# A decoder layer step on one core: the decay's columns loaded once, sums by one product, and the past rows of the FFN in small loads

## The chip, the cores and the metric

The kernel runs on one core of a Trainium2 chip. A core has a matrix engine (TensorE, PE in the profile, with its weight loads shown apart as PEld), a vector engine (VectorE, DVE), a scalar engine (ScalarE, ACT), a general engine (GpSimd, POOL) and a sync engine (SP) that here only issues transfers. Each engine runs its instructions in the order in which they stand in its queue, and waits on semaphores where it needs another engine's result or a transfer. Transfers run on 16 DMA engines and are issued from the queues of SP, POOL and ACT. The metric is the time of one execution on the device in microseconds; the kernel before has a median of 2003.5 us over three runs.

## What is computed

One layer of a hybrid decoder for two request groups that share the weights: a prompt of 256 tokens and 8 samples of one token each, 264 columns together, with a model width of 2048. The reference, cut to what matters here:

```python
proj = jnp.einsum('bld,de->ble', x, w_in)
q, k, v, g, a_lr, cb, cc, ch, mq, z_a, z_b, z_m = jnp.split(proj, SPLIT_POINTS, axis=-1)
log_a = jax.nn.log_sigmoid((a_lr @ w_gla_a2 + b_gla_a2).astype(f32)) / GLA_GATE_NORM   # decay, rank 16
o, s_gla_new = _gla_recurrence(qh, kh, vh, log_a..., s_gla)          # 4 heads, state 256 x 512 each
...
u, s_conv_new = _causal_dwconv(cc * ch, s_conv, w_conv)
...
logits = jnp.einsum('blhd,bmhd->bhlm', qm, mem_k) * (MEM_HD ** -0.5) # 256 memory tokens, 4 heads
p = jax.nn.softmax(logits, axis=-1)
om = jnp.einsum('bhlm,bmhd->blhd', p, mem_v)
...
x = _layer_norm(DN_ALPHA * x + merged @ w_o, ln1_g, ln1_b)
hg = x @ w_ffn_gate; hu = x @ w_ffn_up
hc, s_new = _causal_dwconv(hg, s_ffn, w_ffn_conv, b_ffn_conv)        # s_ffn: 2 past rows of 5504 per sample
x = _layer_norm(DN_ALPHA * x + (jax.nn.silu(hc) * hu) @ w_ffn_down, ln2_g, ln2_b)
```

For the prompt the memory's keys and values are computed from `mem_prompt` and are outputs as well; for the samples they come from a cache, and so do the state of the linear attention and the past rows of the convolutions.

## The kernel before

The activations stand transposed: 128 features on the partitions, 264 tokens along the free dimension. Every float32 operand is split in a high and a low part of a shorter format (fp32r), and a product is made as three: high by high, high by low, low by high (L302, L303, L304). `group` (L280) computes 512 output columns from 16 tiles of 128 input features. Its weights come in tiles of 128 x 1024 values (512 KB): `granule` (L260) loads one on SP's queue into one of four buffers `ws`, ScalarE rounds it to `wh` and VectorE subtracts to `wl` (L277), three buffers each. A `ws` buffer is free for the next load when VectorE has made `wl`; a `wh` buffer when TensorE is through with it. A granule of `group` holds 24 products.

Beside this stream other work is threaded in. `put` queues a unit with its load (one sample's cache or state) and its work; `tick` runs at the end of each granule, counts a clock, runs what `later(n, f)` put off by n ticks, and takes units from the queue. A scheduler then orders each engine's instructions by priorities. `issue_after` orders two instructions on one engine without making one wait for the other.

In order of time, the stages that the change and the prediction speak of:

- **Start.** `constants` (L123) builds on POOL, among other things, `strip`, a table of 32 x 32 identities from which `quads(c)` takes 128 columns.
- **Memory keys and values** (L510 to L542). Two products of the prompt's memory, 512 columns at a time (L520 to L522). Beside them run the samples' key units (`key_unit`, L425): each loads a cache tile of 512 KB and a query row that is spread over 128 partitions from `dq` in DRAM (256 KB), and VectorE multiplies and sums them in four instructions (L439). The results go out on POOL (L529).
- **Attention of the prompt over the memory** (L547 to L578), in two halves of two heads (`c`), each in two tiles of tokens (`lt`): logits on TensorE (L554), maximum and its scaling on VectorE (L557, L558), exponentials on ScalarE (L561), reciprocal and division on VectorE (L563, L564), four transposes on TensorE (L568), then the products with the values (L575).
- **The decay's columns.** `w_in` has 16 columns for the decay (`A0`, with the 16 next to them loaded too). The group at L591 takes them three times, so that the three parts of the second product stand on partitions 0 to 31, 32 to 63 and 64 to 95: three loads of 128 KB for each half of the 2048 features, 48 products of 96 columns. `aT` and `wa2` hold the operands of the second product (L620), 96 partitions each.
- **Samples' sums** (`sum_rows`, L459). For values and for each head's state, VectorE transposes and reduces blocks of 32 x 32 for each of 8 samples into `R`, then `product` adds over the partitions: four products of 32 columns with `quads` (L473) and one copy (L474). This happens six times. `own_key` (L635) sums over 256 channels in two products (L638), once for each head.
- **The FFN's past rows** (L1055 to L1068). `fr`, 86 partitions of 8 x 128, is loaded by POOL in two loads of 172 KB each (L1059): for each of the two past rows, 43 partitions of 8 samples by 128 values. POOL issues them ahead of its next work, in the stage with the `w_conv_out` products (about 850 us). `turn_fpast` turns them on TensorE (L1064) during the products with `w_o`, 20 and 24 ticks after these start.

The order around the change is set by SP's queue (all weight tiles, units and query rows in one line), by VectorE's queue (splits of weights, key units and the softmax in one line), and by which buffers are free.

Of the kernel before, what the change touches and what calls it, by code (L numbers as in the profile page):

```python
# [17 lines left out]
P = 128  # L18
# [16 lines left out]
def layer_kernel(ctx, tc, x_prompt, x_sample, mem_prompt, cache_mem_k, cache_mem_v, state_gla, state_conv,  # L35
# [81 lines left out]
    strip = sb.tile([P, 7 * 32], F32, name="strip")  # L117
    vcol = sb.tile([P, NV], F32, name="vcol")
    fcol = sb.tile([P, 172], F32, name="fcol")

    quads = lambda c: strip[:, 96 - 32 * c:224 - 32 * c]

    def constants():  # L123
        G.memset(strip, 0.0)
        for a in range(4):
            G.tensor_tensor(strip[:, 96:128], strip[:, 96:128], ident[:, 32 * a:32 * a + 32], ALU.add)
# [332 lines left out]
    def sum_rows(sums, b, z, dst, after=None):  # L459
# [9 lines left out]
        def product():  # L469
            pt = small()  # L470
            o = pt[:, 0:4 * NS].rearrange("p (b j) -> p b j", b=NS)
            for c in range(4):
                T.matmul(o, quads(c), R.rearrange("p b (j c) -> p b j c", c=4)[:, :, :, c], start=(c == 0), stop=(c == 3))  # L473
            V.tensor_copy(dst() if callable(dst) else dst, pt[:, 0:4 * NS].rearrange("p (b j) -> p j b", b=NS))  # L474
            if after:
                after()
# [32 lines left out]
    for name, w, dst in (("k", w_mem_k[0], o_mk), ("v", w_mem_v[0], o_mv)):  # L509
# [18 lines left out]
        for m in range(2):  # L528
            G.dma_start(dst[0, 0, m * P:(m + 1) * P].rearrange("m h d -> m (h d)"), mt_[m])  # L529
# [48 lines left out]
    flush()  # L578
# [7 lines left out]
    wr = big(F32, (96, 1024))  # L586
    wa2 = big(F32R, (96, 1024))
    G.memset(wr, 0.0)
    for i in range(3):
        G.dma_start(wr[32 * i:32 * i + 16], w_gla_a2[0])  # L590
    pa, = group([(win, A0, 32)] * 3, 16, xh, xl, gk=8)  # L591
    aT = sb.tile([96, NT], F32R, name="aT")
    S.copy(aT, pa[0:96])
# [17 lines left out]
    def head(h, q, k, vf):  # L611
# [16 lines left out]
        def decays_of_samples():  # L628

            S.activation(eas[:, h], la[:, :, NP:NT], AF.Exp, scale=1.0 / 16.0)  # L630
            dot = tiny((P, 2, NS))
            V.tensor_mul(dot, qks[:, 0, h], qks[:, 1, h])
            later(1, lambda: (V.tensor_mul(qas[:, h], qks[:, 0, h], eas[:, h]), own_key(dot)))

        def own_key(dot):  # L635
            pz = small()
            for kt in range(2):
                T.matmul(pz[:, 0:NS], onesm, dot[:, kt], start=(kt == 0), stop=(kt == 1))  # L638
# [419 lines left out]
    for u in range(2):  # L1058
        G.dma_start(fr[u * NF:(u + 1) * NF], state_ffn_conv[0, :, u].rearrange("b (k f) -> k b f", f=P))  # L1059
# [7 lines left out]
    later(20, lambda: turn_fpast(0))  # L1067
    later(24, lambda: turn_fpast(4))  # L1068
# [333 lines left out]
```

## Time and profile before

| | |
|---|---|
| runs of before | 2004.73, 2000.65, 2003.50 us; median 2003.5 |
| the profiled execution | 2005.06 us, of which the profile's span is 2003.3 us |
| mean granted clock of TensorE | 0.996 |
| DMA | 439 MB in 235199 packets, mean 219 GB/s |
| SP's queue | 426.86 MB, 68.9% of 16 engines |
| POOL's queue | 8.79 MB, 1.3% of 16 engines |
| products of `group`, all three kinds | 14688, of 284 to 287 ns each, which overlap |
| splits of weights (L277) | 651 on ACT, 1039 ns each; 651 on DVE, 1234 ns each |

The profile is of one execution. A row of a timeline gives the start and the length of an instruction in us, its engine, line, operation and operands, and in brackets how long its engine stood idle before it and what ended that. A row of the table of waits reads: engine, operand and line, then what it waited for, the total in us, how often, and the longest. "Granted clock" is the share of full speed that TensorE was given in a stretch. The mean lengths of products overlap, so the time that one costs is read from how many start in a stretch.

### The profile page before, as it was taken

What the parts mean: (1) busy time and instruction counts of PE and PEld (TensorE: products, weight loads), DVE (VectorE), ACT (ScalarE), POOL (GpSimd) and SP (SyncE); (2) the same over time, 40 slices, a digit from 0 to 9 for tenths busy, and PEclk for the clock granted to TensorE, in tenths of its full rate; (3) what the DMA queues carried; (4) which work ended last, traced back from release to release, by engine and by line L of the source; (5) the groups of instructions that cost most, each with busy time, mean ns of one, the idle gap of its engine ahead of it and who ended that gap; (6) DMA issues with size and microseconds to landing.
All of it is one profiled execution on the core that took longest, in us unless ns stands there. A gap on an engine that the chain in (4) does not pass through costs nothing.

```text
span 2003.3 us, 38161 instructions
## 1 busy us (share of the span) xinstructions
PE 1984.9 (99%) x15721; PEld 1950.6 (97%) x15721; DVE 1296.7 (65%) x1947; ACT 986.3 (49%) x1348; POOL 164.1 (8%) x240
## 2 busy tenths in 40 slices
PE   9998999999999999999999999999999999999998
PEld 9887999999999999999999998999999999999997
DVE  5675866566676867865444787666665556666655
ACT  4433654454554555554444346555554445555533
POOL 4000030021310211100000201000000000000100
PEclk9999999999999999999999999999999999999999
DMA  8895866566666667866555567877777787777753
GB/s 282 272 316 189 274 201 198 176 211 197 189 190 195 201 190 241 259 173 183 179 179 181 178 213 252 256 236 231 233 246 249 259 254 238 232 233 247 237 177 119
DMA packets 235199, 439.00 MB, mean 219 GB/s; under 512 B 22862, under 2 KB 29571, under 8 KB 234889
## 3 DMA queue, kind: packets, MB, share of 16 engines
q1 hardware_dynamic: 229120, 426.86, 68.9%
q0 software_dynamic: 5040, 8.79, 1.3%
q8 instruction: 123, 2.02, 0.4%
q10 hardware_dynamic: 864, 0.92, 0.1%
q14 instruction: 52, 0.42, 0.1%
HBM read 409.76 MB, written 26.90 MB: 218 GB/s over the span
## 4 chain that ended last, share of the span: by engine, by line
PE 72%; DVE 1%; ACT 0%; issue 0%; DVEq 0%; ACTq 0%
PE mm L303 23%; PE mm L302 23%; PE mm L304 23%; PE sm L803 1%; PE sm L679 0%; PE sm L781 0%; DVE G L935 0%; PE sm L473 0%; PE sm L1276 0%; DVE wl L277 0%; PE sm L849 0%; PE sm L783 0%; PE bank L1331 0%; PE mm L1139 0%; ACT wh L277 0%
## 5 line engine op out<-in xcount | busy, mean ns | idle before, releaser
L277 DVE TENSOR_TENSOR wl<-ws,wh 128x1024 fp32r<-128x1024 f32 (+2 forms) x651 | 802.6, 1234 | 582.0 <-ACT wh L277 580.2
L277 ACT CAST wh<-ws 128x1024 fp32r<-128x1024 f32 (+2 forms) x651 | 676.1, 1039 | 878.0 <-PE mm L303 770.0
L302 PE MATMUL mm<-XH,wh 128*128 128x264 f32 (+1 forms) x2064 | 592.8, 287 | 1.8 <-ACT wh L277 1.0
L303 PE MATMUL mm<-XL,wh 128*128 128x264 f32 (+1 forms) x2064 | 588.8, 286 | 0.0
L304 PE MATMUL mm<-XH,wl 128*128 128x264 f32 (+1 forms) x2064 | 586.2, 285 | 0.7 <-DVE wl L277 0.7
L302 PE MATMUL mm<-T,wh 128*128 128x264 f32 x1456 | 415.1, 285 | 0.0
L303 PE MATMUL mm<-T,wh 128*128 128x264 f32 x1456 | 414.2, 284 | 0.0
L304 PE MATMUL mm<-T,wl 128*128 128x264 f32 x1456 | 413.8, 284 | 0.0
L302 PEld LDWEIGHTS mm<-XH,wh 128*128 128x128 f32 (+1 forms) x2064 | 390.0, 189 | 2.7 <-ACT wh L277 1.2
L302 PE MATMUL mm<-X1H,wh 128*128 128x264 f32 x1376 | 391.5, 284 | 0.0
L303 PE MATMUL mm<-X1L,wh 128*128 128x264 f32 x1376 | 391.1, 284 | 0.0
L304 PE MATMUL mm<-X1H,wl 128*128 128x264 f32 x1376 | 391.0, 284 | 0.0
L303 PEld LDWEIGHTS mm<-XL,wh 128*128 128x128 f32 (+1 forms) x2064 | 389.4, 189 | 0.5 <-DVE XL L317 0.2
L304 PEld LDWEIGHTS mm<-XH,wl 128*128 128x128 f32 (+1 forms) x2064 | 387.8, 188 | 1.2 <-DVE wl L277 1.0
L302 PEld LDWEIGHTS mm<-T,wh 128*128 128x128 f32 x1456 | 274.1, 188 | 0.1
L303 PEld LDWEIGHTS mm<-T,wh 128*128 128x128 f32 x1456 | 274.0, 188 | 0.1
L304 PEld LDWEIGHTS mm<-T,wl 128*128 128x128 f32 x1456 | 273.8, 188 | 0.0
L302 PEld LDWEIGHTS mm<-X1H,wh 128*128 128x128 f32 x1376 | 259.4, 189 | 0.2 <-issue 0.2
L303 PEld LDWEIGHTS mm<-X1L,wh 128*128 128x128 f32 x1376 | 259.0, 188 | 0.2 <-DVE T L1160 0.2
L304 PEld LDWEIGHTS mm<-X1H,wl 128*128 128x128 f32 x1376 | 258.4, 188 | 0.0
L1080 POOL DMA_DIRECT2D out_dram<-S x2 | 1.1, 551 | 637.2 <-DVE S L1077 637.2
L521 PE MATMUL mm<-wl,T 128*128 128x512 f32 x128 | 50.6, 395 | 0.0
(363 smaller groups left out, 1485.7 us busy)
## 6 DMA issues: line engine op xcount, KB each, us to landing
ws<-in_w_in_dram SPq DMA_DIRECT2D x255, 512.0 KB, 4.0
ws<-in_w_ffn_down_dram SPq DMA_DIRECT2D x84, 512.0 KB, 4.8
ws<-in_w_ffn_gate_dram SPq DMA_DIRECT2D x80, 512.0 KB, 4.4
ws<-in_w_ffn_up_dram SPq DMA_DIRECT2D x80, 512.0 KB, 4.7
S<-in_state_gla_dram SPq DMA_DIRECT2D x64, 512.0 KB, 5.3
ws<-in_w_gla_out_dram SPq DMA_DIRECT2D x32, 512.0 KB, 3.7
ws<-in_w_o_dram SPq DMA_DIRECT2D x32, 512.0 KB, 4.2
out_dram<-S SPq DMA_DIRECT2D x32, 512.0 KB, 4.2
```

Of the source, the lines that this page charges most:

```text
L277: split_at[:] = [S.copy(wh, st).ins, V.tensor_sub(wl, st, wh.bitcast(F32)).ins]
L302: T.matmul(p, wh[:, t, cs], xh(kt), start=(kt == 0), stop=False)
L303: T.matmul(p, wh[:, t, cs], xl(kt), start=False, stop=False)
L304: i = T.matmul(p, wl[:, t, cs], xh(kt), start=False, stop=(kt == nk - 1))
L521: T.matmul(pts[m], a, wl[:, t], start=False, stop=False)
L803: T.matmul(pt, kd[:, st, kt * P:(kt + 1) * P], vt[:, st], start=(st == 0), stop=(st == 1))
L1080: G.dma_start(o_pffn[0, 0, u].rearrange("(k f) -> k f", f=P), rows[:, 0])
```

## The change

The decay's columns are loaded once for each half of the features (two loads of 128 KB in place of six). ScalarE writes the high part three times side by side, VectorE the low part as a fourth block of 32 columns. A tile of features then takes two products: the 128 columns by the high part of x, and the first 96 by its low part. `aT` and `wa2` have 128 partitions, and `wr` is loaded a fourth time.

In `sum_rows` one product of 128 columns, with a table `modulo` of four identities side by side, replaces the four; four copies, on DVE and ACT in turn, pick each group of 32 partitions out of its result. `modulo` is built by VectorE from `ident`, and `strip` with its work on POOL goes. `own_key` adds its two halves on VectorE and makes one product.

The past rows are loaded on SP: sixteen loads of 43 rows of 512 B, for one sample and one past row each, two of them behind each of eight weight tiles from the first `w_o` group on, and they are turned 14 and 18 ticks after its start. The memory's keys and values are written 2 and 8 ticks later (`later`), and the loop after the attention empties the queue of units alone.

```diff
-    strip = sb.tile([P, 7 * 32], F32, name="strip")
+    modulo = sb.tile([P, 4, 32], F32, name="modulo")
-    quads = lambda c: strip[:, 96 - 32 * c:224 - 32 * c]
     def constants():
-        G.memset(strip, 0.0)
-        for a in range(4):
-            G.tensor_tensor(strip[:, 96:128], strip[:, 96:128], ident[:, 32 * a:32 * a + 32], ALU.add)
+        i4 = ident.rearrange("p (a i) -> p a i", a=4)
+        V.tensor_add(modulo[:, 0:2], i4[:, 0:2], i4[:, 2:4])
+        V.tensor_add(modulo[:, 3], modulo[:, 0], modulo[:, 1])
+        V.tensor_copy(modulo[:, 0:3], modulo[:, 3:4].to_broadcast([P, 3, 32]))
...
         def product():
             pt = small()
-            o = pt[:, 0:4 * NS].rearrange("p (b j) -> p b j", b=NS)
+            T.matmul(pt[:, 0:P], modulo.rearrange("p a i -> p (a i)"), R.rearrange("p b c -> p (b c)"),
+                     start=True, stop=True)
+            d = dst() if callable(dst) else dst
             for c in range(4):
-                T.matmul(o, quads(c), R.rearrange("p b (j c) -> p b j c", c=4)[:, :, :, c], start=(c == 0), stop=(c == 3))
-            V.tensor_copy(dst() if callable(dst) else dst, pt[:, 0:4 * NS].rearrange("p (b j) -> p j b", b=NS))
+                own = pt[32 * c:32 * c + 32, 0:P].rearrange("p (b j c) -> p j b c", b=NS, c=4)[:, :, :, c]
+                (S.copy if c % 2 else V.tensor_copy)(d[32 * c:32 * c + 32], own)
...
         for m in range(2):
-            G.dma_start(dst[0, 0, m * P:(m + 1) * P].rearrange("m h d -> m (h d)"), mt_[m])
+            later(2 + 6 * m, lambda dst=dst, mt_=mt_, m=m: G.dma_start(
+                dst[0, 0, m * P:(m + 1) * P].rearrange("m h d -> m (h d)"), mt_[m]))
...
-    flush()
+    while queue:
+        pop()
...
-    wr = big(F32, (96, 1024))
-    wa2 = big(F32R, (96, 1024))
+    wr = big(F32, (P, 1024))
+    wa2 = big(F32R, (P, 1024))
     G.memset(wr, 0.0)
-    for i in range(3):
+    for i in range(4):
         G.dma_start(wr[32 * i:32 * i + 16], w_gla_a2[0])
-    pa, = group([(win, A0, 32)] * 3, 16, xh, xl, gk=8)
-    aT = sb.tile([96, NT], F32R, name="aT")
-    S.copy(aT, pa[0:96])
+    pa = ps.tile([P, 512], F32, tag="mm", bufs=5, name=nm("mm"))[:, :NT]
+    for g in (0, 8):
+        lead[0] += 1
+        with tc.high_priority(offset=700):
+            st = sb.tile([P, 8, 32], F32, tag="ws", bufs=4, name=nm("ws"))
+            staged[:] = [nc.sync.dma_start(
+                st, win[g * P:(g + 8) * P, A0:A0 + 32].rearrange("(k p) c -> p k c", p=P)).ins]
+        with tc.high_priority(offset=450):
+            wa = sb.tile([P, 8, P], F32R, tag="wh", bufs=3, name=nm("wh"))
+            split_at[:] = [S.copy(wa[:, :, 0:96].rearrange("p k (a c) -> p k a c", a=3),
+                                  st.unsqueeze(2).to_broadcast([P, 8, 3, 32])).ins,
+                           V.tensor_sub(wa[:, :, 96:P], st, wa[:, :, 0:32].bitcast(F32)).ins]
+        for t in range(8):
+            kt = g + t
+            if kt:
+                T.matmul(pa[0:96], wa[:, t, 0:96], xl(kt), start=False, stop=False)
+            i = T.matmul(pa, wa[:, t], xh(kt), start=(kt == 0), stop=(kt == 15))
+            if kt == 0:
+                T.matmul(pa[0:96], wa[:, t, 0:96], xl(kt), start=False, stop=False)
+        last_mm[:] = [i.ins]
+        tick(1 - g // 8, 2)
+    aT = sb.tile([P, NT], F32R, name="aT")
+    S.copy(aT, pa)
...
+            V.tensor_add(dot[:, 0], dot[:, 0], dot[:, 1])
...
-            for kt in range(2):
-                T.matmul(pz[:, 0:NS], onesm, dot[:, kt], start=(kt == 0), stop=(kt == 1))
+            T.matmul(pz[:, 0:NS], onesm, dot[:, 0], start=True, stop=True)
...
-    for u in range(2):
-        G.dma_start(fr[u * NF:(u + 1) * NF], state_ffn_conv[0, :, u].rearrange("b (k f) -> k b f", f=P))
+    def load_fpast(b):
+        with tc.issue_after(staged[0]):
+            for u in range(2):
+                nc.sync.dma_start(fr[u * NF:(u + 1) * NF, b], state_ffn_conv[0, b, u].rearrange("(k f) -> k f", f=P))
+    for b in range(NS):
+        later(1 + b, lambda b=b: load_fpast(b))
...
-    later(20, lambda: turn_fpast(0))
-    later(24, lambda: turn_fpast(4))
+    later(14, lambda: turn_fpast(0))
+    later(18, lambda: turn_fpast(4))
```

Three queues at the end of the memory's values, as the built programs have them. First SP, from the last weight tile of the memory's values (`ws_1635`, after the change `ws_1633`) to the query row of the last key unit (`T_292`); tiles of 128x8x32 are the decay's columns, `S` is a key unit's cache tile. Before:

```order
L270 DMA ws_1635<-in_w_mem_v_dram 128x2x512
L430 DMA T_263_1445<-dq 128x512
L270 DMA ws_1786<-in_w_in_dram 128x8x32 x3
L428 DMA S_282_1531<-in_cache_mem_k_dram 128x2x512
L270 DMA ws_1818<-in_w_in_dram 128x8x32 x3
L270 DMA ws_1866<-in_w_in_dram 128x2x512
L430 DMA T_283_1533<-dq 128x512
L270 DMA ws_1896<-in_w_in_dram 128x2x512
L428 DMA S_291_1561<-in_cache_mem_k_dram 128x2x512
L270 DMA ws_1926<-in_w_in_dram 128x2x512
L270 DMA ws_1974<-in_w_in_dram 128x2x512
L430 DMA T_292_1563<-dq 128x512
```

After:

```order
L269 DMA ws_1633<-in_w_mem_v_dram 128x2x512
L429 DMA T_263_1442<-dq 128x512
L601 DMA ws_1783<-in_w_in_dram 128x8x32
L427 DMA S_282_1529<-in_cache_mem_k_dram 128x2x512
L429 DMA T_283_1531<-dq 128x512
L601 DMA ws_1804<-in_w_in_dram 128x8x32
L427 DMA S_291_1559<-in_cache_mem_k_dram 128x2x512
L269 DMA ws_1842<-in_w_in_dram 128x2x512
L429 DMA T_292_1561<-dq 128x512
```

The last query row stands behind one large weight tile where it stood behind four, and behind two of the narrow loads where there were six.

Second VectorE, from the key unit with `T_283` to the reciprocal of the first softmax tile or as far as twelve rows go; `ls` takes a key unit's sums, `wl` is the low part of a weight tile, `ty` the softmax's maximum, `sm_1662` and `sm_1658` its logits. Before:

```order
L439 SCALAR_TENSOR_TENSOR T_302_1607,ls<-S_282_1531,T_283_1533 128x256
L557 TENSOR_REDUCE ty_1667<-sm_1662 128x2
L439 SCALAR_TENSOR_TENSOR T_306_1627,ls<-S_291_1561,T_292_1563 128x256
L439 SCALAR_TENSOR_TENSOR T_307_1629,ls<-S_291_1561,T_292_1563 128x256
L439 SCALAR_TENSOR_TENSOR T_308_1631,ls<-S_291_1561,T_292_1563 128x256
L439 SCALAR_TENSOR_TENSOR T_309_1633,ls<-S_291_1561,T_292_1563 128x256
L558 TENSOR_SCALAR ty_1667<-ty_1667 128x2
L277 TENSOR_TENSOR wl_1899<-ws_1896,wh_1898 128x1024
L563 RECIPROCAL ty_1667<-ty_1667 128x2
```

After:

```order
L607 TENSOR_TENSOR wh_1785<-ws_1783,wh_1785 128x8x32
L438 SCALAR_TENSOR_TENSOR T_306_1625,ls<-S_291_1559,T_292_1561 128x256
L438 SCALAR_TENSOR_TENSOR T_307_1627,ls<-S_291_1559,T_292_1561 128x256
L438 SCALAR_TENSOR_TENSOR T_308_1629,ls<-S_291_1559,T_292_1561 128x256
L438 SCALAR_TENSOR_TENSOR T_309_1631,ls<-S_291_1559,T_292_1561 128x256
L607 TENSOR_TENSOR wh_1806<-ws_1804,wh_1806 128x8x32
L529 COPY T_215_1265<-mm_1465 128x512
L276 TENSOR_TENSOR wl_1845<-ws_1842,wh_1844 128x1024
L560 TENSOR_REDUCE ty_1663<-sm_1658 128x2
L561 TENSOR_SCALAR ty_1663<-ty_1663 128x2
L276 TENSOR_TENSOR wl_1875<-ws_1872,wh_1874 128x1024
L566 RECIPROCAL ty_1663<-ty_1663 128x2
```

The last key unit stood between the softmax's maximum and its scaling; it now stands ahead of the second split of the decay's columns (`wh_1806`), of the copy of the memory's values and of the whole softmax.

Third TensorE, from the last decay products (`mm_1785`, after the change `mm_1782`) to the logits of the second softmax tile; `mm_1862` and `mm_1838` to `mm_1840` belong to the first group of q. Before:

```order
L304 MATMUL mm_1785<-XH,wl_1823 96x264
L302 MATMUL mm_1862<-XH,wh_1868 128x264
L568 MATMUL sm_1675<-ident,T_320_1670 128x128 x4
L554 MATMUL sm_1681<-T_209_1243,T_46_428 128x256 x4
L303 MATMUL mm_1862<-XL,wh_1868 128x264
```

After, from the last three of the thirteen products that now stand there:

```order
L302 MATMUL mm_1839<-XL,wh_1844 128x264
L303 MATMUL mm_1839<-XH,wl_1845 128x264
L301 MATMUL mm_1840<-XH,wh_1844 128x264
L571 MATMUL sm_1671<-ident,T_320_1666 128x128 x4
L557 MATMUL sm_1677<-T_209_1239,T_46_428 128x256 x4
```

Between the decay's products and the softmax's transposes stood one product of the group of q; now there are thirteen.

## The prediction

> **What bounds the kernel now.** I read the page's busy times and its chain first, to see which engine sets the end.
>
> ```profile
> span 2003.3 us, 38161 instructions
> PE 1984.9 (99%) x15721; PEld 1950.6 (97%) x15721; DVE 1296.7 (65%) x1947; ACT 986.3 (49%) x1348; POOL 164.1 (8%) x240
> PE 72%; DVE 1%; ACT 0%; issue 0%; DVEq 0%; ACTq 0%
> ```
>
> TensorE is busy for 1984.9 of 2003.3 us, and the chain that ended last is nearly all TensorE. So an edit can pay in two ways only: fewer TensorE instructions, or a shorter stall out of the 18.4 us in which PE is idle. The table of windows says where those are.
>
> ```profile
> 120.00:200.00 80.00, 73.19 (x397) 64.15 (x396) 47.23 (x111) 28.25 (x49) 3.48 (x6) 0.96 0.73 233
> 1240.00:1900.00 660.00, 660.00 (x5426) 660.00 (x5425) 402.99 (x593) 344.82 (x486) 7.28 (x8) 1.00 0.78 243
> 1980.00:2004.00 24.00, 15.89 (x111) 13.22 (x109) 11.48 (x32) 6.00 (x15) 0.00 (x0) 0.83 0.27 91
> ```
>
> The columns are the stretch, its length, busy time (count) of PE, weight loads, DVE, ACT and POOL, then granted clock, DMA share, GB/s. From 1240 to 1900 nothing is idle: 660 us / 5426 = 0.1216 us for one product of 264 columns, the price of a TensorE instruction below. 8.1 us are idle in the tail, which the change does not touch, 6.8 between 120 and 200. The waits of PE name the causes.
>
> ```profile
> PE sm L568 <- ACT wh L277: 6.3, 1, 6.3
> PE mm L302 <- ACT wh L277: 1.0, 1, 1.0
> PE mm L304 <- DVE wl L277: 0.7, 1, 0.7
> ```
>
> One wait of 6.3 us stands at the softmax of the memory attention (about 161 to 167). The other two are one stall of 1.7 us at 873.5 to 876. The change works at both.
>
> **The decay's columns: products.** The group of L591 ran 48 products.
>
> ```profile
> 154.65 0.47 PE L302 MATMUL mm<-XH,wh 128*96 128x264 f32 x1
> 160.57 0.28 PE L304 MATMUL mm<-XH,wl 128*96 128x264 f32 x1
> ```
>
> 47 steps in 5.92 us are 0.126 us each, so 96 columns cost about what 128 do. 32 products remain: 16 x 0.1216 = **-1.95 us**. The wider aT, wa2 and the fourth POOL load lie on engines that are idle there.
>
> **The decay's columns: the 6.3 us stall.** Releasers are inferred, so I looked for what was late.
>
> ```profile
> 139.10 2.77 SPq L270 DMA_DIRECT2D ws<-in_w_in_dram  x3
> 142.59 5.72 SPq L270 DMA_DIRECT2D ws<-in_w_in_dram  x4
> 152.81 0.46 SPq L430 DMA_DIRECT2D T<-dq  x1
> 143.41 1.22 DVE L277 TENSOR_TENSOR wl<-ws,wh 128x1024 fp32r<-128x1024 f32 x1 [1.54 <-ACT wh L277]
> 153.22 0.42 DVE L439 SCALAR_TENSOR_TENSOR T<-S,T 128x256 f32<-128x256 f32 x1 [0.26 <-DMA T<-dq]
> 154.88 1.23 DVE L277 TENSOR_TENSOR wl<-ws,wh 128x1024 fp32r<-128x1024 f32 x1 [0.88 <-ACT wh L277]
> 163.57 0.42 DVE L439 SCALAR_TENSOR_TENSOR T<-S,T 128x256 f32<-128x256 f32 x1 [6.18 <-DMA T<-dq]
> 164.96 0.16 DVE L558 TENSOR_SCALAR ty<-ty 128x2 f32<-128x2 f32 x1
> 165.16 0.47 ACT L561 ACTIVATE T<-sm,ty 128x256 f32<-128x256 f32 x1 [6.24 <-DVE ty L558]
> 167.25 1.09 PE L568 MATMUL sm<-ident,T 128*128 128x128 f32 x4 [6.28 <-ACT wh L277]
> ```
>
> The last key unit's query row (dq) was issued at 152.81 and landed at 163.5, 10.7 us later. VectorE waited 6.18 us for it with the softmax (L558) queued behind; then ScalarE, then TensorE. On SP that load stood behind several large weight tiles, and the last two of these had to wait for buffers. The order now puts it behind one, ws_1842, whose buffer is freed by the split of ws_1607, the row at 143.41, which ends at 144.6. So it is issued at about 145.1, 7.7 us sooner. Its landing takes between 4.9 us (issued at the end of the x4 row, 148.3; waited for until 153.2) and 10.7 us: at 150.0 or 155.8. I take 150, as four of the six narrow loads ahead are gone. The last key unit's 1.5 us and both small splits (L607) are then done by about 152, before TensorE needs the second one (154.65 + 16 x 0.12 = 156.6).
>
> What is late next: the softmax itself. The split at 154.88 ends at 156.1. Reduction 0.7, then 2.3 (from the scale at 164.96 to the transposes at 167.25), then 1.6 more, since an exponential and a weight cast of 1.05 now stand between the two halves: transposes at 160.7. TensorE arrives there at 154.65 + 45 x 0.1216 = 160.1 (32 decay and 13 further products). 0.6 us are left, and by the same count 0.5 at the second tile. Stall: -6.3 + 1.1 = **-5.2 us**. The stall also halved the clock:
>
> ```profile
> 166.00:168.00 2.00, 0.76 (x4) 0.79 (x5) 1.06 (x3) 1.38 (x4) 0.00 (x0) 0.52 1.02 343
> 168.00:170.00 2.00, 2.00 (x7) 1.64 (x6) 1.63 (x2) 0.00 (x0) 0.00 (x0) 0.50 0.86 294
> 170.00:172.00 2.00, 2.00 (x8) 1.64 (x7) 0.41 (x2) 0.00 (x0) 0.00 (x0) 0.50 0.39 67
> 172.00:174.00 2.00, 2.00 (x15) 2.00 (x15) 1.07 (x3) 0.78 (x3) 0.00 (x0) 0.77 0.60 214
> ```
>
> 2 x (0.48 + 0.50 + 0.50 + 0.23) = 3.4 us, less 0.6 for the idle part of the first row: **-2.8 us**.
>
> **Samples' sums and own keys.**
>
> ```profile
> 579.70 0.82 PE sm L473 x8
> 576.32 0.44 PE sm L679 x4
> 657.21 0.34 PE sm L638 x4
> ```
>
> Each of six sums drops from four products (0.82) to one of 128 x 128, half of the second row: 0.22. 6 x 0.60 = **-3.6 us**. The four own keys halve the third row: 4 x 0.17 = **-0.7 us**. DVE pays four small adds and 12 copies, ACT 12 copies. Each costs about 0.2 us (a copy below); DVE is 65% and ACT 49% busy, so at nothing, until a copy holds up a weight cast.
>
> ```profile
> 881.35 0.19 DVE L474 COPY T<-sm 128x32 f32<-128x32 f32 x1 [2.61 <-PE sm L473]
> 1129.90 1.05 ACT L277 CAST wh<-ws 128x1024 fp32r<-128x1024 f32 x1 [1.90 <-PE mm L303]
> ```
>
> In the worst case a copy waits 2.6 us on ACT as here; a cast is made two tiles (5.8 us) before TensorE needs it and with its split takes 2.3, so 3.5 us are spare.
>
> **The FFN's past rows.** Their two POOL loads explain the stall at 873. First row: the two loads. Second: weight loads issued from 849 to 873. Third: weight loads of w_o, 1110 to 1160, undisturbed.
>
> ```profile
> S<-in_state_ffn_conv_dram POOLq DMA_DIRECT2D x2, 172.0 KB, 19.5
> ws<-in_w_in_dram SPq DMA_DIRECT2D x7, 512.0 KB, 11.8
> ws<-in_w_o_dram SPq DMA_DIRECT2D x16, 512.0 KB, 4.2
> 873.90:877.00 3.10, 1.50 (x6) 1.29 (x7) 2.11 (x3) 2.42 (x3) 0.00 (x0) 0.85 0.08 29
> 877.00:880.00 3.00, 3.00 (x18) 3.00 (x17) 1.67 (x2) 0.48 (x1) 0.00 (x0) 0.59 0.89 224
> ```
>
> While they run, weights take 11.8 us instead of 4.2. From 873.9 to 877 the DMA share is 0.08, about one engine of 16, at 29 GB/s (26 in a steady slice): one engine still owes its part of a weight tile, and TensorE waits. The loads leave this place, so **-1.7 us** stall and, from the clocks 0.85 and 0.59, 3.1 x 0.15 + 3.0 x 0.41 = **-1.7 us**.
>
> They come back as 16 loads of 43 rows of 512 B on SP, two behind each of eight w_o tiles from about 1126. What one costs no row shows. Two rows bound it: POOL's loads alone (853.75 to 856.5), and 128-byte pieces on SP's queue (146.5 to 149); packets, MB, share of 16 engines.
>
> ```profile
> q0 software_dynamic: 391, 0.06, 17.7%
> q1 hardware_dynamic: 1544, 0.20, 55.6%
> ```
>
> POOL's two loads kept 0.177 x 16 = 2.8 engines busy, 20 ns a packet, of which the two loads need 1376 (two to a row): 40 ns x 43 = 1.7 us a load if it runs on one engine. From below, 22 KB at 26 GB/s is 0.85. Between: 14.4 ns for 128 B (second row) and 79 ns for 2 KB at 26 GB/s give 27 ns for 512 B, 1.2 us a load. I take 1.2, since that row is of the same queue. Per w_o tile (24 x 0.1216 = 2.92 us) one engine would then carry 2.4 us of past rows and 1.26 of weights (32.8 KB at 26 GB/s), 0.7 too much, 5.9 us over eight tiles. Cover: a buffer comes free 9.4 us before its next cast (four tiles less 2.3) and the load takes 4.2, so 5.2, plus the 3.5 above: 8.7. So nothing; at 1.7 us a load it is 14 - 8.7 = 5 us of stall. A rule of the Trainium skill speaks against the change here: "DMA: Bandwidth & Descriptors", section "Why a DMA increments its semaphore by 16 and not by 1", says that a load is split over as many engines, up to 16, as divide its slowest dimension on both sides, and that on SP's queue these are the lowest-numbered ones; 43 gives one, the same for all sixteen loads. The share of 2.8 engines for two loads is nearer to that than to 16 each, and no run here shows which engine SP takes; by the rule rival 1 is what threatens, and without it (loads on several engines) there is no lag at all. The sum is the same by both.
>
> **At nothing.** The shorter turn (14, 18 ticks), the output loads put off by `later` (POOL's order is the same as before, and its waits too), and the table built on DVE, which waits there anyway:
>
> ```profile
> 6.00 0.89 DVE L317 TENSOR_TENSOR XL<-sm,XH 128x512 fp32r<-128x512 f32 x2 [4.37 <-ACT XH L317]
> ```
>
> **Sum.** 1.95 + 5.2 + 2.8 + 3.6 + 0.7 + 3.4 = 17.65 us. The profiled execution took 2005.06 us, 1.56 above the median 2003.5; so 1987.4 by the profile, **1986 us** for the median.
>
> **Rivals.**
> 1. Past rows pile up on one engine at 1.7 us a load: 5 us of stall near 1140 to 1155, perhaps 2.6 of clock. For it: the 11.8 us above. Against: spread over 23 us and behind the weights. 1991 to 1994. On the clock: the skill ("TensorE: Matmul & The Clock Gate", section "HAM oscillation — how this bites in real kernels") wants a gap over some 3.4 us before the clock falls, so it would keep these 2.6; the stall at 873, with 1.7 us idle, fell to 0.59, and disagrees.
> 2. The query row takes 10.7 us wherever it is issued and lands at 155.8. VectorE's order now has the second decay split behind it, so key unit, split, copy (0.7) and weight split end at about 159.6, 3.5 us later, less the overlap with TensorE's queue, about 3, and 1.7 of clock: 1991.
> 3. The 873 stall is not the past rows' doing and stays: 1986 + 3.4 = 1989.4.
> 4. **Slower.** Rival 1 in the extreme: TensorE starves in w_o for the whole gain. It decides where the lag exceeds 17.65 + 8.7 = 26 us, 3.3 a tile, a load over (2.92 + 3.3 - 1.26) / 2 = 2.5 us, 58 ns a row. POOL's rows took 40, so it needs a slower queue than any row shows. At 3 us a load: (6 + 1.26 - 2.92) x 8 = 35 us less 8.7, some 2012.
> 5. The change doesn't do what it says: both stalls stay, with only the 6.25 us of products gained and small new waits against them: 1997 to 2003.
>
> **How the numbers follow.** Forecast 0.60; rival 1 0.12; rival 2 0.10; rival 3 0.06; rival 5 0.06; rival 4 0.06. What a measurement of this kernel can tell from no change is about 0.2%, 4 us. Faster by more: the first four, 0.88. Within: 0.06. Slower: 0.06. The range 1982 to 1994 reaches from the sum without any leftover (another 1.1) and the 2.9 us by which a run before lay under the median, to rivals 1 and 2; 0.12 is left out.
>
> **What would show it.** Right: PE's wait at the softmax under 1.5 us and a granted clock of 1.00 from 160 to 180; no wait near 873; 32 products for the decay; six products of 0.22 us. The load of the last query row near 145. Wrong: PE waiting for weights between 1130 and 1160 with a DMA share near 0.06; VectorE waiting for T<-dq ahead of the second L607; a wait that moved to the value units after 200.

## The result and the profile after

| | before | after |
|---|---|---|
| six runs, us | 2004.73, 2000.65, 2003.50, 2001.54, 2001.75, 2003.67 | 1986.95, 1986.66, 1988.05, 1987.24, 1990.27, 1987.60 |
| median, us | 2002.62 | 1987.42 |
| the profile's span, us | 2003.3 | 1985.2 |

The ratio is 0.9926, with a 95% interval of 0.9913 to 0.9939: 15.2 us less. Forecast were 1986.0 us (1982 to 1994), that is 17.5 us less than the median of 2003.5 that was known then. The spans of the two profiled executions lie 18.1 us apart. One execution of the run `bearly700` below took 2122.73 us at a granted clock of 0.85, where its others had 0.996 to 0.998, and is left out of that run's ratio.

The page of the changed kernel, its head and TensorE's busy time:

```profile
span 1985.2 us, 38068 instructions
PE 1973.5 (99%) x15661; PEld 1939.0 (98%) x15661; DVE 1297.7 (65%) x1960; ACT 987.5 (50%) x1360; POOL 159.0 (8%) x234
```

TensorE's busy time fell by 11.4 us (1984.9 to 1973.5), its idle time by 6.7 (18.4 to 11.7). Busy time also holds what a lower clock costs, so the two halves of a stall turn up in different sums. The table of windows and the table of PE's waits show where the idle time went:

```profile
120.00:200.00 80.00, 78.98 (x467) 70.07 (x466) 54.63 (x123) 34.89 (x61) 3.97 (x7) 1.00 0.76 246
860.00:880.00 20.00, 20.00 (x165) 19.93 (x165) 16.00 (x25) 12.18 (x20) 0.00 (x0) 1.00 0.63 177
```

```profile
PE sm L571 <- DVE T L567: 0.5, 2, 0.3
PE mm L301 <- DVE G L1010: 0.5, 1, 0.5
...
PE sm L571 <- ACT wh L276: 0.4, 2, 0.2
```

Between 120 and 200 TensorE is idle for 1.0 us instead of 6.8, at a granted clock of 1.00 instead of 0.96. The wait of 6.3 us at the softmax's transposes (L568 before, L571 now) is down to 0.9 in four pieces, and no weight cast is waited for near 860 (873 before, now some 15 us earlier). The timelines of SP, VectorE, ScalarE and TensorE around the softmax, first SP's loads (the second column is the time that the issue took), then the others:

```profile
144.52 0.47 SPq L429 DMA_DIRECT2D T<-dq  x1
149.62 0.43 DVE L438 SCALAR_TENSOR_TENSOR T<-S,T 128x256 f32<-128x256 f32 x1 [1.23 <-DMA T<-dq]
151.00 0.42 DVE L607 TENSOR_TENSOR wh<-ws,wh 128x256 fp32r<-128x256 f32 x1
156.43 0.47 ACT L564 ACTIVATE T<-sm,ty 128x256 f32<-128x256 f32 x1 [2.20 <-PE mm L612]
156.89 1.04 ACT L276 CAST wh<-ws 128x1024 fp32r<-128x1024 f32 x1
157.83 0.47 ACT L564 ACTIVATE T<-sm,ty 128x256 f32<-128x256 f32 x1
160.13 0.63 PE L571 MATMUL sm<-ident,T 128*128 128x128 f32 x4 [0.29 <-DVE T L567]
```

The last query row is issued at 144.52 (152.81 before) and used at 149.62 (163.57 before): 5.1 us for a landing that took 10.7. VectorE waits for it 1.23 us instead of 6.18, and both splits of the decay's columns (L607) are done at 151.4. The two exponentials stand apart by a weight cast, as the prediction had it, and the transposes run at 160.13 after a wait of 0.29.

One of the six sums, in the chain that ended last, and an own key with the instruction behind it, in TensorE's timeline:

```profile
567.26 0.22 PE sm L471 x2
```

```profile
643.90 0.28 PE L663 MATMUL sm<-ty,onesm 128*128 128x8 f32 x2
644.03 1.07 PE L689 MATMUL sm<-ident,T 128*128 128x128 f32 x8
```

A sum takes 0.22 us where it took 0.82; an own key 0.13 (from 643.90 to 644.03) where it took 0.34, or 0.36 counted in the same way (657.05 to 657.41). SP's timeline, the first and the last pair of past rows, and the windows in which they land:

```profile
1089.03 0.70 SPq L1087 DMA_DIRECT2D S<-in_state_ffn_conv_dram  x2
...
1110.66 2.36 SPq L1087 DMA_DIRECT2D S<-in_state_ffn_conv_dram  x2
```

```profile
1105.00:1110.00 5.00, 5.00 (x43) 5.00 (x43) 4.22 (x9) 2.86 (x4) 0.00 (x0) 1.00 0.67 210
1110.00:1115.00 5.00, 5.00 (x43) 5.00 (x42) 1.88 (x2) 1.91 (x2) 0.00 (x0) 1.00 0.45 139
```

The issue of a pair grows from 0.70 to 2.36 us, perhaps because a queue behind it fills up, which no run varied; TensorE stays busy all through.

### The profile page after: what moved, and what is told of

It reads as the page before. It is cut to its first block, busy times and chain, and to the rows that moved or that the text cites. A ratio compares the mean times of both kernels' runs of the same rounds, so it can differ in the third digit from the quotient of the medians.

```text
span 1985.2 us, 38068 instructions
## 1 busy us (share of the span) xinstructions
PE 1973.5 (99%) x15661; PEld 1939.0 (98%) x15661; DVE 1297.7 (65%) x1960; ACT 987.5 (50%) x1360; POOL 159.0 (8%) x234
## 4 chain that ended last, share of the span: by engine, by line
PE 72%; DVE 1%; ACT 0%; issue 0%; DVEq 0%; ACTq 0%
PE mm L302 23%; PE mm L301 23%; PE mm L303 23%; PE sm L828 1%; PE sm L704 0%; DVE wl L276 0%; PE sm L806 0%; DVE G L960 0%; PE sm L1307 0%; PE sm L874 0%; PE sm L808 0%; PE bank L1362 0%; ACT L651 0%; DVE G L1010 0%; PE mm L1170 0%
## 5 line engine op out<-in xcount | busy, mean ns | idle before, releaser
L301 PE MATMUL mm<-XH,wh 128*128 128x264 f32 x2048 | 586.5, 287 | 0.7 <-DVE G L1010 0.5
L302 PE MATMUL mm<-XL,wh 128*128 128x264 f32 x2048 | 583.3, 285 | 0.0
L303 PE MATMUL mm<-XH,wl 128*128 128x264 f32 x2048 | 580.4, 284 | 0.0
L301 PEld LDWEIGHTS mm<-XH,wh 128*128 128x128 f32 x2048 | 386.2, 189 | 1.3 <-DVE G L1010 0.7
L302 PEld LDWEIGHTS mm<-XL,wh 128*128 128x128 f32 x2048 | 385.5, 188 | 0.5 <-DVE XL L316 0.2
L303 PEld LDWEIGHTS mm<-XH,wl 128*128 128x128 f32 x2048 | 384.0, 188 | 0.4 <-DVE wl L276 0.2
```

Of the source, the lines that this page charges most:

```text
L301: T.matmul(p, wh[:, t, cs], xh(kt), start=(kt == 0), stop=False)
L302: T.matmul(p, wh[:, t, cs], xl(kt), start=False, stop=False)
L303: i = T.matmul(p, wl[:, t, cs], xh(kt), start=False, stop=(kt == nk - 1))
```

## The experiments

Twelve further runs were made. In the first series one part of the change was undone, in the second one part alone was put into the kernel before; then single causes were varied. The medians in one series share the runs of the kernel before.

**The changed kernel again.**

> The changed kernel once more, beside the same runs of before as the three kernels with one part undone. Theory A (the gain is the sum of the parts): about 1987 us, a ratio to before of 0.992 to 0.993, no wait of TensorE at the softmax over 0.5 us, none between 840 and 900. Theory B (the two stalls come and go from execution to execution, whatever the code): the profile shows one of the two stalls here, 2 to 9 us.

Measured: 1987.09 us against 2001.17 (ratio 0.9932, 0.9919 to 0.9944), span 1985.5, TensorE without idle time between 840 and 900. Its waits at the softmax's transposes add up to 1.1 us, the longest of them 0.5. Theory A holds. The kernel before spread from 1995.88 to 2005.01 in these twelve runs, the changed one from 1986.40 to 1988.88 in five.

**The decay undone.** The group of `(win, A0, 32)` three times with `gk=8`, as in the kernel before, in the changed kernel:

```diff
-    pa = ps.tile([P, 512], F32, tag="mm", bufs=5, name=nm("mm"))[:, :NT]
-    for g in (0, 8):
-        ...
+    pa, = group([(win, A0, 32)] * 3, 16, xh, xl, gk=8)
```

> The changed kernel with the decay's columns loaded three times and 48 products again. Theory A: 16 products back (1.95 us), and the last query row stands behind six narrow loads and four weight tiles on SP again, so that the wait at the softmax (4 to 6 us) and the half clock behind it (2 to 3 us) come back: 1995 to 1998 us. Theory B (that stall is not this part's): 1.95 us alone, 1989.4 us, and no wait over 1 us at the softmax.

Measured: 1996.51 us, 9.4 more than the changed kernel of the same series (ratio to before 0.9976, 0.9965 to 0.9988). PE's waits and the window behind them:

```profile
PE sm L571 <- ACT wh L276: 5.4, 1, 5.4
```

```profile
160.00:180.00 20.00, 14.33 (x80) 12.95 (x80) 10.81 (x25) 5.78 (x15) 0.00 (x0) 0.83 0.60 194
```

The stall is back with 5.4 us, and a clock of 0.83 over 20 us with it. Theory A.

**The decay alone,** the same block put into the kernel before.

> The kernel before with only the decay part (loaded once, two products for each tile of features). Theory A: 1.95 us of products, about 5 us of the wait at the softmax and 2.8 us of half clock go: 10 us, 1992.6 us, and the stall near 873 stays (1 to 2 us with its half clock). Rival (the wait at the softmax needs the later writes of the memory's keys and values too): 1.95 us, 2000.7 us.

Measured: 1991.49 us against 2001.54: 10.05 us less (ratio 0.9952, 0.9940 to 0.9965), clock 1.00 from 160 to 180. Forecast for this part were 1.95 + 5.2 + 2.8 = 9.95. The later writes of the memory's keys and values and the emptied queue are not needed for it. This kernel still has the past rows on POOL, and the stall that goes with them, in its waits and windows:

```profile
PE mm L304 <- DVE wl L277: 0.7, 1, 0.7
...
PE mm L302 <- ACT wh L277: 0.4, 1, 0.4
```

```profile
862.50:865.00 2.50, 1.52 (x11) 1.09 (x9) 1.10 (x1) 1.76 (x2) 0.00 (x0) 1.00 0.40 150
865.00:867.50 2.50, 2.32 (x19) 2.32 (x20) 2.29 (x4) 1.38 (x2) 0.00 (x0) 1.00 0.53 138
```

It is 1.1 us long here, and the clock stays at 1.00. The profile also has a wait that neither profile of the kernel before has: 1.4 us at L521, among the products of the memory's values (118 to 122), where the clock stays at 1.00 too. Without it this part would have gained more, so that the agreement of 10.05 with 9.95 is in part luck.

**Only the loads of the decay made three times.** 32 products and the new splits stay; two of the three copies are read by nothing.

```diff
-            st = sb.tile([P, 8, 32], F32, tag="ws", bufs=4, name=nm("ws"))
+            sw = sb.tile([P, 8, 96], F32, tag="ws", bufs=4, name=nm("ws"))
+            st = sw[:, :, 0:32]
+            for r in range(3):
+                staged[:] = [nc.sync.dma_start(
+                    sw[:, :, 32 * r:32 * r + 32], win[...].rearrange("(k p) c -> p k c", p=P)).ins]
```

> The changed kernel with each narrow load of the decay's columns made three times (two copies that nothing reads); its 32 products and its splits stay. With them the scheduler puts the last query row behind four large weight tiles and six narrow loads again. Theory A (the loads and what they move on SP's queue make the stall): a wait of 4 to 6 us and a half clock of 2 to 3 us come back, 1993.5 to 1996.5 us. Rival (the 48 products or the splits made it): no wait over 1 us at the softmax, 1987.4 us.

Measured: 1994.92 us against 2001.54 (ratio 0.9970, 0.9959 to 0.9981). PE's waits, a window, SP's narrow loads and last query row, and VectorE at the last two query rows:

```profile
PE mm L303 <- DVE wl L276: 4.7, 1, 4.7
PE sm L571 <- DVE T L567: 2.5, 3, 2.1
```

```profile
165.00:180.00 15.00, 11.36 (x59) 10.15 (x59) 9.98 (x20) 4.02 (x10) 0.00 (x0) 0.66 0.58 200
```

```profile
138.64 2.99 SPq L603 DMA_DIRECT2D ws<-in_w_in_dram  x3
142.36 5.01 SPq L603 DMA_DIRECT2D ws<-in_w_in_dram  x3
...
152.04 0.55 SPq L429 DMA_DIRECT2D T<-dq  x1
```

```profile
153.28 0.42 DVE L438 SCALAR_TENSOR_TENSOR T<-S,T 128x256 f32<-128x256 f32 x1 [0.89 <-DMA T<-dq]
164.51 0.42 DVE L438 SCALAR_TENSOR_TENSOR T<-S,T 128x256 f32<-128x256 f32 x1 [7.34 <-DMA T<-dq]
```

So the stall needs neither the 48 products nor the old splits: the loads, and the place on SP to which they move the last query row, make it. It stands partly ahead of the transposes now, at a weight split. The six narrow loads keep SP issuing for 8.0 us, the two of the changed kernel for 0.7 (0.37 each); the difference, 7.3 us, is about the 7.5 us by which the last query row is issued later (152.04 against 144.52).

**The last query row earlier, all else as before.** The priority of the last sample's loads is raised; the scheduler then puts the last query row ahead of two of the four large tiles.

```diff
+            with tc.high_priority(offset=700 if b == NS - 1 else 0):
                 nc.sync.dma_start(kc, cache_mem_k[...])
                 nc.sync.dma_start(pb, dq[...].to_broadcast([P, 512]))
```

> The kernel before, nothing changed but the priority of the last sample's two key loads and query rows, so that the last query row stands ahead of two of the four large weight tiles on SP; all six narrow loads and 48 products stay. Theory A (the row is late because of where it stands in the queue): issued some 3 us sooner, the wait of VectorE for it and of TensorE at the softmax 3 us or more shorter, the half clock shorter too: 1996 to 1999.5 us. Rival (the narrow loads' many small packets set when it lands, wherever it stands): it lands at about 163 again, 2002.6 us.

Measured: 1999.42 us against 2001.54 (ratio 0.9990, 0.9981 to 0.9999), 2 us less, and the interval only just leaves out no change. The kernel ran once more, for its profile:

> The kernel of the run bearly700 again, for a profile that is not disturbed. Theory A (the row is late because of where it stands on SP): the last query row issued at 149 to 150 instead of 152.8, and the waits of VectorE for it and of TensorE at the softmax 3 us or more shorter than 6.2 and 6.3. Rival (the many small packets ahead set when it lands): VectorE waits for it until about 163 again.

Measured: 1998.81 us in one run. SP, VectorE, and PE's wait:

```profile
148.32 0.98 SPq L431 DMA_DIRECT2D T<-dq  x1
157.00 0.43 DVE L440 SCALAR_TENSOR_TENSOR T<-S,T 128x256 f32<-128x256 f32 x1 [0.66 <-DMA T<-dq]
```

```profile
PE sm L569 <- DVE T L565: 4.2, 3, 3.8
```

The row is issued at 148.32 and lands at 157.0, 8.7 us later; before, it was issued at 152.81 and landed at 163.5, 10.7 us later. VectorE's wait goes from 6.18 to 0.66. TensorE's waits at the softmax's transposes go from 6.7 us in all to 4.5 only (7.7 in the second profile of before, below): the key units ahead still come late, and the softmax behind them. Theory A holds for the row; of the 3 us or more that it gave TensorE's wait, 2.2 to 3.2 are there. So the place in the queue is a part of the cause. The six narrow loads ahead of all the rows, which this run leaves in place, may be the rest; it doesn't part the two.

**The samples' sums and own keys undone.**

```diff
-            T.matmul(pt[:, 0:P], modulo..., R..., start=True, stop=True)
+            for c in range(4):
+                T.matmul(o, quads(c), R...[:, :, :, c], start=(c == 0), stop=(c == 3))
+            V.tensor_copy(dst() if callable(dst) else dst, ...)
```

> The changed kernel with four products of 32 columns for each of the six sums of the samples, one copy, and the own keys in two products each again. Theory A: 6 x 0.60 and 4 x 0.17 us of TensorE come back: 4.3 us, 1991.7 us. Rival: the twelve copies on ScalarE and twelve on VectorE that go with it gave part of that away by holding up weight casts: then less than 4.3 us comes back, 1988 to 1990 us, though TensorE's busy time grows by 4.3.

Measured: 1990.31 us, 3.2 more than the changed kernel (ratio to before 0.9949, 0.9937 to 0.9962); the spans differ by 3.6. The pages' busy times, first the changed kernel again, then this one:

```profile
PE 1974.0 (99%) x15661; PEld 1939.4 (98%) x15661; DVE 1297.7 (65%) x1960; ACT 987.5 (50%) x1360; POOL 159.4 (8%) x234
```

```profile
PE 1977.3 (99%) x15705; PEld 1944.1 (98%) x15705; DVE 1295.5 (65%) x1947; ACT 986.1 (50%) x1348; POOL 160.3 (8%) x239
```

TensorE's busy time grew by 3.3 us, not by 4.3, so the missing 1.1 us is not a wait that the copies cause. The 44 instructions that come back account for 4.3 by their rows. What gives the rest back these profiles don't show, and an uncertainty of some 2.5 us on the ratio covers it.

**The past rows undone,** POOL's two loads at the old place in the changed kernel.

```diff
-    for b in range(NS):
-        later(1 + b, lambda b=b: load_fpast(b))
+    for u in range(2):
+        G.dma_start(fr[u * NF:(u + 1) * NF], state_ffn_conv[0, :, u].rearrange("b (k f) -> k b f", f=P))
```

> The changed kernel with the FFN's past rows in POOL's two loads at the old place again. Theory A: a wait of TensorE for a weight cast of 1 to 2 us some 20 us after the two loads are issued, and a half clock behind it of about as much: 1990 to 1991 us. Rival: the stall at 873 belonged to something else in the kernel before, nothing comes back: 1987.4 us, or some tenths less without sixteen loads on SP.

Measured: 1987.18 us against 1987.09: nothing (ratio to before 0.9933, 0.9920 to 0.9945). The answer on the two loads, issued at 834.8 and 837.5, and the window in which the second one lands:

```profile
DMA to landing us min/median/max: 14.7/17.0/19.2
```

```profile
848.00:858.00 10.00, 10.00 (x84) 10.00 (x84) 5.62 (x8) 3.04 (x4) 0.00 (x0) 1.00 0.82 227
```

The loads land 2.5 us sooner than in the kernel before, and TensorE never waits. In the changed kernel this part of the change is worth nothing, as the rival forecast; its reason, that the stall belonged to something else, is another matter, which the next run bears on.

**The past rows alone,** on SP in the kernel before.

> The kernel before with only the past rows moved to SP behind eight w_o tiles. Theory A: 3.4 us go (1.7 of wait and 1.7 of half clock near 873), 1999.2 us, with the wait at the softmax as before. Rival (the stall near 873 is not the past rows' doing): no change, 2002.6 us, stall still there.

Measured: 2001.06 us against 2001.54 (ratio 0.9993, 0.9984 to 1.0002). Neither forecast fits whole. The stall near 873 is gone, as the window shows, and the wait at the softmax is there, but the time is not 3.4 us shorter. PE's waits and the window:

```profile
PE sm L568 <- ACT wh L277: 6.6, 1, 6.6
...
PE mm L521 <- DVE wl L277: 1.1, 1, 1.1
```

```profile
870.00:890.00 20.00, 20.00 (x165) 19.93 (x165) 12.63 (x20) 11.47 (x17) 0.00 (x0) 1.00 0.61 181
```

The wait of 1.1 us at L521 lies among the products of the memory's values, which this change doesn't touch; it is the one that the run with the decay alone has (1.4 us).

**The kernel before again,** for a second profile.

> The kernel before once more, for a second profile of it. Theory B2 (the size of its two stalls differs from execution to execution, and the execution profiled first was one with both large): the wait at the softmax 5 to 7 us again, the one near 873 between 0 and 1.5 us and without a half clock behind it; span 1997 to 2001 us. Rival (both stalls are always as in the first profile, and moving the past rows costs elsewhere what it saves): 1.7 us and a half clock near 873 again, span about 2003 us.

Measured: 2001.67 us, span 1999.9. PE's waits and the window:

```profile
PE sm L568 <- ACT wh L277: 7.0, 1, 7.0
...
PE mm L304 <- DVE wl L277: 0.8, 1, 0.8
```

```profile
870.00:880.00 10.00, 9.03 (x73) 8.60 (x72) 5.80 (x8) 5.28 (x5) 0.00 (x0) 1.00 0.66 207
```

The wait at the softmax is there again. The stall near 873 is 1.0 us of idle time here (10 - 9.03) without a lower clock, where the first profile had 1.7 us and 1.7 us of half clock: 1.0 us against 3.4.

**The price of a past row on SP.** Two runs: the sixteen loads all asked for at the first w_o tile,

```diff
-        later(1 + b, lambda b=b: load_fpast(b))
+        later(1, lambda b=b: load_fpast(b))
```

> The changed kernel with all sixteen loads of past rows behind the first w_o tile instead of two behind each of eight. If one DMA engine carries them all, one after the other at 27 ns a row (1.16 us a load, from the packets in the trace of the changed kernel), it owes 18.6 us while the next weight tiles need it too; against 8.7 us of cover TensorE waits some 10 us in all for weights between 1090 and 1130, and some us of half clock come on top: 1997 to 2001 us. Rival (the loads spread over the sixteen engines, 1.2 us on each): no wait there, 1987.2 us.

Measured: 1987.10 us against 2001.97 (ratio 0.9927, 0.9910 to 0.9944), one wait for a weight cast of 0.4 us, in the first 60 us, and TensorE without idle time from 1085 to 1160. But the scheduler did not pile them up: three loads, or two, stand behind each of six tiles, so the forecast of 10 us had a queue in mind that did not come to be. The packets in the trace tell the price all the same:

```text
512-byte packets of SP's queue, 1085 to 1140: 688, 27 ns each (median)
started per microsecond while they run: 42 or 43, never more
weights' packets (2048 bytes) in the same stretch: 84 ns (median)
```

One row begins every 23.5 ns (a microsecond over 42.5 rows), and a row takes 27: they pass nearly one after the other, as through one engine at a time; which engine, the trace doesn't name. A weight tile's 512 KB are 256 packets, 16 for each engine if they are spread evenly. Then every load was made twice, the second time into a tile that nothing reads:

```diff
-                nc.sync.dma_start(fr[u * NF:(u + 1) * NF, b], ...)
+                for to in (fr, spare):
+                    nc.sync.dma_start(to[u * NF:(u + 1) * NF, b], ...)
```

> The changed kernel with every load of past rows made twice (the second into a tile that nothing reads): 32 loads, three behind each of some eleven w_o tiles. By the packets of the run pile one load keeps one engine for 43 x 23.5 ns = 1.0 us and a weight tile for 16 x 84 ns = 1.3 us, so this engine has 4.4 us of work for every 2.92 us of TensorE and falls behind by 1.5 us a tile, 16 us in all. If the cover is 8.7 us as the prediction worked out, TensorE waits about 7 us for weights before 1125, with 0 to 3 us of half clock: 1994 to 1997 us. Rival (the cover is longer, or the loads don't share one engine with the weights): no wait, 1987.2 us.

Measured: 1994.88 us against 2001.49 (ratio 0.9970, 0.9959 to 0.9982), 7.8 us more than the changed kernel. PE's waits; ScalarE's timeline of weight casts; VectorE's with the sum at L1162; the windows:

```profile
PE mm L301 <- DVE T L1162: 3.2, 1, 3.2
...
PE mm L303 <- DVE wl L276: 0.8, 1, 0.8
```

```profile
1117.64 1.05 ACT L276 CAST wh<-ws 128x1024 fp32r<-128x1024 f32 x1 [3.33 <-DMA ws<-in_w_o_dram]
1120.95 1.05 ACT L276 CAST wh<-ws 128x1024 fp32r<-128x1024 f32 x1 [2.26 <-DMA ws<-in_w_o_dram]
1125.26 1.05 ACT L276 CAST wh<-ws 128x1024 fp32r<-128x1024 f32 x1 [3.27 <-DMA ws<-in_w_o_dram]
1129.60 1.04 ACT L276 CAST wh<-ws 128x1024 fp32r<-128x1024 f32 x1 [3.29 <-DMA ws<-in_w_o_dram]
```

```profile
1130.68 1.22 DVE L276 TENSOR_TENSOR wl<-ws,wh 128x1024 fp32r<-128x1024 f32 x1 [2.77 <-ACT wh L276]
1131.82 1.10 DVE L1162 SCALAR_TENSOR_TENSOR T<-T,mm 128x264 f32<-128x264 f32 x3
```

```profile
1125.00:1130.00 5.00, 3.26 (x23) 2.62 (x21) 1.56 (x2) 1.45 (x2) 0.00 (x0) 1.00 0.63 205
1130.00:1135.00 5.00, 2.70 (x12) 2.71 (x13) 4.29 (x6) 1.69 (x2) 0.00 (x0) 0.61 0.34 117
1135.00:1140.00 5.00, 5.00 (x30) 4.93 (x29) 2.34 (x3) 1.05 (x1) 0.00 (x0) 0.70 0.82 274
```

Now the weight tiles come as slowly as one engine delivers: 3.31 us apart (1117.64 to 1120.95) with two loads between them, 4.31 and 4.34 with three. The difference is the price of a load, 1.0 us, and 3.31 - 2 x 1.0 = 1.3 us is the engine's part of a weight tile, as the packets gave. Only 0.8 us of TensorE's wait is for a weight split. The other 3.2 end with a sum on VectorE (L1162), three of whose four steps stand in VectorE's queue behind the split of a late tile (1130.68), which waited 2.77 us for its cast. By the price the engine falls behind by 16 us, TensorE waits 4.0, so the cover is some 12 us, an estimate; the expectation had 8.7. Of the other 3.8 us the lower clock makes 2.6 (5 x 0.39 + 5 x 0.30, less 0.9 for the idle part); 1.2 are not accounted for.

## Why the prediction was right, and where it was not

The time, 1987.42 us, lies in the range, 1.4 us above the forecast. By its steps:

1. **The decay, 9.95 us forecast: 10.05 alone, 9.4 when undone.** Each instant of the chain came out within 0.6 us: issue of the row "at about 145.1" (144.52), landing at 150.0 (149.62), both splits done "by about 152" (151.4), TensorE at the transposes at 160.1 (159.84, which is 160.13 less the wait of 0.29), the transposes at 160.7 (160.13), 1.1 us of stall left (0.9). The choice of the short landing, 4.9 us, over 10.7 was right (5.1), and rival 2 falls. The reason given for it, four narrow loads fewer ahead, is not shown, and the rows speak against it as it stands: the row that took 4.9 us in the kernel before came after all six narrow loads in SP's order, and with the loads tripled in the changed kernel the same row takes 5.2 (148.08 to 153.28). The last row differs from it by three large weight tiles and a cache tile, 512 KB each, that stand between the two; it lands 10.4 us after it in the kernel before (153.22 to 163.57) and 11.2 with the loads tripled. In the run with the row earlier one such tile stands between, and it lands 2.1 us after the other (154.88 to 157.00). What the narrow loads are seen to do is to make the issue late. So the value was right by luck as far as the narrow loads are its reason; which of the other transfers of that time make the landing long was not varied. The granted clock from 120 to 200 is 1.00, so the 2.8 us of half clock went with the stall.
2. **Sums and own keys, 4.3 us forecast: 3.2 by the medians, 3.3 by busy time.** The sums' rows are as forecast (0.82 to 0.22), and no copy held up a weight cast on TensorE's path. The term was too large by 1.1 us, within the interval of the run, and the profiles don't say why.
3. **The past rows, 3.4 us forecast: 0.5 alone (between 3.2 less and 0.4 more by the interval), none when undone.** This is the step that failed. The mechanism was half right. With the past rows alone on SP the wait of TensorE near 873 is gone, and with the two loads on POOL it is there in four of the five profiles with a mean clock over 0.99 (1.7 and 1.0 us in the kernel before, 1.1 with the decay alone, 0.8 with the row earlier). But it is not there in the fifth, the changed kernel with these loads on POOL, so that the loads are needed for the stall and don't suffice. And the prediction put it down at its size in one execution, 1.7 us and another 1.7 of half clock; the second profile of the kernel before has 1.0 and no half clock. The profiled execution took longer, at 2005.06 us, than any of the first six runs, and "1.56 above the median" should have warned that one of its stalls might be longer than usual. Rival 3 had this term at nothing, which is nearly what came, though not for its reason: it had the loads as no part of the cause.
4. **The sixteen loads at nothing: right, with the price as taken.** 1.2 us a load was an estimate from two rows; 1.0 is measured, on one engine. The upper bound of 1.7 us rested on a misreading: POOL's 1376 packets are not two for each row of 512 B but, by the sizes in the trace, 86 of 4096 B with the data and 1290 of 32 B. Two loads and a tile's part need 3.31 us against 2.92, a lag of 0.4 us for each of eight tiles, 3 us in all, against a cover of some 12; the prediction had 5.9 against 8.7. So rival 1 and the slower rival 4 fall. With twice as many loads a stall like rival 1's comes (7.8 us in all), but not the loss of the whole gain that rival 4 had. The rule of the Trainium skill that the prediction weighed ("DMA: Bandwidth & Descriptors", section "Why a DMA increments its semaphore by 16 and not by 1") gives one engine for 43 rows, and the packets agree (42 or 43 start in a microsecond, never more). Only the place was off: the loads stand at 1089 to 1113 and not from about 1126, since w_o's tiles are loaded four buffers ahead of their products.
5. **The sum.** By the medians of the experiments 10.05 + 3.2 + 0.1 to 0.5 gives 13.3 to 13.8 us, beside 14.1 measured in the same series and 15.2 in the first comparison. The forecast's 17.65 was 3.4 us too large from step 3 and 1.1 from step 2. The time forecast is closer than that, 1.4 us, because the median that it started from, 2003.5, was 0.9 above the six runs' and 1.5 to 2.3 above those of the later series. So two errors partly cancelled, which is luck.

What stays open: why POOL's two loads land in 14.7 and 19.2 us in the changed kernel with these loads on POOL, and later in the four profiles that have the stall (16.6 to 17.2 and 20.9 to 21.7). A different queue is not the reason: counted from the issue of POOL's first load, SP's transfers of weights and of the samples' state from 38 us ahead of it to 12 us behind it stand in the same order and at the same places in all five, within 0.8 us, and from 12 us ahead within 0.1. Also not varied was a landing of the last query row between 4.9 and 10.7 us with the narrow loads kept small.

## What to carry to other kernels

A wait that stands in every profile of a kernel with the six narrow loads in their old place (6.3, 7.0, 6.6 and 5.4 us at the softmax) may be counted at its size; one of a microsecond near the end of its cover has to be seen in a second profile first, since it may be there, halve the clock or vanish by how a transfer happens to land. Where a late transfer ends a wait, its place in the queue, the time that the issues ahead of it take and the large transfers just before it are the first to look at: dropping four narrow loads of 128 KB saved 8 us of stall and lower clock, though nothing on TensorE's own list pointed at them. A small load whose rows went through one engine here cost that engine's time for the weights too; count its microseconds per weight tile, and compare the lag with the cover.

## What the runs showed of the hardware

- The clock fell behind 1.7 us of idle time within 2.5 us (before, 873.5 to 876), not behind 1.0 (before again), nor behind 1.1 near 865 and 1.4 from 118 to 122 (decay alone). Behind 4.0 us in two pieces, the longer of them 3.2 (loads twice), it was 0.61 from 1130 to 1135 and 0.70 from 1135 to 1140. The Trainium skill ("TensorE: Matmul & The Clock Gate", section "HAM oscillation — how this bites in real kernels") wants a gap over some 3.4 us. The first profile of before disagrees, and loads twice, with 3.2, is just under it.
- A row of 512 B on SP's queue took 27 ns and the next began after 23.5; by this 43 of them hold one engine for 1.0 us, while a tile of 512 KB holds each engine for 1.3 (16 packets of 84 ns).
- SP took 0.37 us to issue one narrow load of 128 KB in the changed kernel, and 2.99 and 5.01 us for three in a row (loads three times); what SP waited for there is not shown.
- Runs of the kernel before spread over 9 us in one series (1995.88 to 2005.01, twelve runs), those of the changed kernel over 2.5 and 3.6 (five and six runs). That the stall makes the difference is not shown: with it back (decay undone) eight runs spread over 3.7.
